# A decoder trunk on one core: x's turns as threads, the last eight weight tiles kept, small products joined

## The chip, the cores and the metric

One core of a Trainium2 chip runs the whole program. The metric is device microseconds per execution: the median of three timed runs. Beside it stands one profiled execution, from which all durations come. The engines are PE (TensorE matmul; PEld is its weight load), DVE (VectorE), ACT (ScalarE), POOL (GpSimd) and SP (SyncE, which here only issues DMAs); each works through its own instructions in program order.

## The reference, cut to what matters

One layer on x of 256 tokens by 2048 channels, all float32:

```python
h = rmsnorm(x, norm_mix_w)
proj = h @ w_in                      # q, k, v, z, b, a, p_in, g_a, g_b
q, k, v = split(silu(causal_dwconv([q, k, v], conv_qkv_w)))
o = gated_delta_rule(l2norm(q), l2norm(k), v, g_log, beta)      # 16 heads of 128
y_a = rmsnorm(o, gdn_norm_w) * silu(z)
y_b = (causal_multiscale_pool(p_in) @ pool_w) * pool_scale
x = x + (sigmoid(g_a) * y_a + sigmoid(g_b) * y_b) @ w_out
gate, up = split(rmsnorm(x, norm_ffn_w) @ w_up)
x = x + (gelu(causal_dwconv(gate, conv_ffn_w) + conv_ffn_b) * up) @ w_down
return rmsnorm(x, norm_final_w)
```

## The kernel before

**The big products.** Every large product is computed in float32 accuracy by three passes of a rounded type: a matrix A is split into a rounded part (hi) and a rest (lo), and hi*hi + lo*hi + hi*lo is summed in PSUM. A weight tile is 256 rows by 512 columns (512 KB). `fetch` (L275) loads it into `raw` (four buffers) on SP's queue, `cast` (L284) makes `whi` on ACT, `split` (L292) makes `wlo` on DVE (`whi` and `wlo` have four buffers each, `wpool`). `weights` (L317) gives the next tile; casts run up to `AHEAD` = 3 tiles in front of the one in use, and fetches up to four tiles in front of the splits. One tile feeds 12 matmuls of 128x512: two k blocks, two token halves (t = 0, 1), three passes. Eight tiles make one product of 2048 by 512 (`gemm_a`, L327), a "step" being one tile.

**The order of the work.** The program's order on each engine is written out by hand, by a small planner at build time. `Plan` (L32) keeps a modelled time for every engine and one for the DMA queue: `dma` (L50) adds a transfer's bytes at 240 KB per us, starting at time 0. Side work is written as generators ("threads"), spawned with a rank; `side` (L205), called after each k block of a big product, first emits what the weight pipeline can do and then the next piece of any thread that the plan holds to be ready. A piece names its engine by `yield "PE"`, `yield "A"` (ACT), `"V"` (DVE), `"G"` (POOL), `"S"` (SP). `until` (L236) repeats this until a condition holds. `bank` (L157) and `leave` hand out the two PSUM buffers `psb`; `pa` gives the two buffers `psa`, `pm` the large ones `psm`.

**The start.** Loads of x (four tiles) and of the first four weight tiles go out alternately (L396 to L401). nmrows, the first norm's weights, is turned on PE into `nmw`. `x_turned` (L411) turns two 128-row blocks of x by four PE transposes, ACT evicts them as `xhi` with the scale, DVE makes `xlo`. `x_turned(0)` is called before the first big product (L1049), and `x_next(c)`, called ahead of step c, calls `x_turned(c + 1)` (L1058): it emits all three engines' parts at once.

**Small products on PE.** In `gdn` (L682; four head groups) the inverse of a triangular block is put together from 32 to 64 to 128 rows: for each of two head pairs (hp) a product `pu` is made on PE, evicted as `u` on ACT, and then the next pair's (L773 and L804). The products that follow (`px`) are made for both pairs at once. `pooled` (L898) multiplies by band matrices, `mixing` (L937) and `residual` (L1105) transpose; each does its work in two halves, PE then ACT then DVE, one bank at a time.

**The end.** The down projection accumulates eight banks: `acc[c][t]`, four column blocks c of 512 and two token halves t. For each row pair kp of 22 and each c, a tile feeds both t (L1232). In the last row pair, c = 0 is done for both halves, then c = 1, 2, 3 for t = 0, then the first half's end is emitted, then c = 1, 2, 3 for t = 1 and the second half's end (L1245 to L1267). An end is: four adds on DVE and four sums of squares on ACT, a reduce and a scale on DVE, a power on POOL (`rs`), scaling by `rs` and by the final weights `nfin` (two columns on DVE, two on ACT), and four stores of 256 KB on SP's queue.

Of the kernel before, what the change touches and what calls it, by code (L numbers as in the profile page):

```python
# [13 lines left out]
P = 128  # L14
# [17 lines left out]
class Plan:  # L32
# [75 lines left out]
def kernel(  # L108
# [163 lines left out]
    def soon(eng, time):  # L272
        return time <= max(now["PE"], now[eng])

    def fetch():  # L275
        i = len(raws)
        src = srcs[i]
        raw = wpool.tile(list(src.shape), F32, tag="raw", name=nm("raw"), bufs=4)
        plan.at(free[i - 4] if i >= 4 else 0.0)
        nc.sync.dma_start(raw, src)  # L280
        landed.append(plan.ready)
        raws.append(raw)

    def cast():  # L284
        i = len(rounded)
        hi = wpool.tile(list(raws[i].shape), F32R, tag="whi", name=nm("whi"))
        plan.at(max(landed[i], now["PE"] if i > AHEAD else 0.0))
        nc.scalar.copy(hi, raws[i])
        cast_at.append(plan.ready)
        rounded.append(hi)  # L290

    def split():  # L292
        i = len(made)
        raw, hi = raws[i], rounded[i]
        plan.at(max(cast_at[i], now["PE"] if i > AHEAD else 0.0))
        if hi.shape[1] == 8:
            lo = None
            nc.vector.tensor_tensor(hi[:, :, 32:64], raw[:, :, 0:32], hi[:, :, 0:32].bitcast(F32), op=ALU.subtract)
        else:
            lo = wpool.tile(list(raw.shape), F32R, tag="wlo", name=nm("wlo"))  # L300
# [95 lines left out]
    for c in range(4):  # L396
# [4 lines left out]
        fetch()  # L401

    plan.at(nmready)
# [5 lines left out]
    xhi, xlo = xhl[:, :, 0, :], xhl[:, :, 1, :]  # L409

    def x_turned(k2):  # L411
        pt = (pa if k2 % 2 else pb)([P, 2, S])
        plan.at(x0[k2 // 2][1])
        for kk in range(2):
            k = 2 * k2 + kk
            for t in range(2):
                nc.tensor.transpose(pt[:, kk, t * P : (t + 1) * P], x0[k // 4][0][:, t, (k % 4) * P : (k % 4 + 1) * P],
                                    ident)
        for kk in range(2):
            k = 2 * k2 + kk  # L420
            nc.scalar.activation(xhi[:, k, :], pt[:, kk, :], AF.Copy, scale=nmw[:, k : k + 1])
        for kk in range(2):
# [259 lines left out]
    def gdn(g, kq, vts, dec0, dec1, res):  # L682
# [88 lines left out]
        pairs = [(slice(o, o + 32), slice(o + 32, o + 64)) for o in (0, 64)]  # L771
        U = []
        for hp in range(2):  # L773
            yield "PE"
            pu = pa([P, 2, 2, 32])
            for t, i in probs:
                for lo, up in pairs:
                    mm(pu[up, t, i, :], lt(2 * hp + i, t)[lo, up], T[hp][lo, t, i, lo], start=True, stop=True)
            u = mp.tile([P, 2, 2, 32], F32, tag="U", bufs=2, name=nm("U"))
            yield "A"  # L780
            for lo, up in pairs:
                nc.scalar.copy(u[up], pu[up])
            U.append(u)
# [18 lines left out]
        lo, up = slice(0, 64), slice(64, 128)  # L802
        U = []
        for hp in range(2):  # L804
            yield "PE"
            pu = pa([P, 2, 2, 64])
            for t, i in probs:
                mm(pu[up, t, i, :], lt(2 * hp + i, t)[lo, up], T[hp][lo, t, i, lo], start=True, stop=True)
            u = mp.tile([P, 2, 2, 64], F32, tag="U", bufs=2, name=nm("U"))
            yield "A"  # L810
            nc.scalar.copy(u[up], pu[up])
            U.append(u)
# [85 lines left out]
    def pooled(e, g, phi, plo):  # L898
        for f2 in range(2):
            yield "PE"  # L900
            n = yield from bank()
            pt = pb([P, 2, S])
            for ff in range(2):
# [3 lines left out]
                mm(pt[:, ff, 0 : P + PAD], e[:, 0, fs], bands[:, g, 0 : P + PAD], start=False, stop=True,  # L907
                   skip_group_check=True)
            fs = slice(2 * f2, 2 * f2 + 2)
            yield "A"  # L910
# [26 lines left out]
    def mixing(g, sz, ps, psb, tb, res, mh, ml):  # L937
# [10 lines left out]
        give("th")  # L948
        for f2 in range(2):
            yield "PE"  # L950
            n = yield from bank()
            pt = pb([P, 2, S])
# [4 lines left out]
            if f2:  # L957
                give("sz")
            fs = slice(2 * f2, 2 * f2 + 2)
# [42 lines left out]
    for g in range(4):  # L1002
# [57 lines left out]

# [44 lines left out]
    def residual(c, ps):  # L1105
# [7 lines left out]
        for k2 in range(2):  # L1113
            yield "PE"
            n = yield from bank()
            pt = pb([P, 2, S])
            for kk in range(2):
                k = 4 * c + 2 * k2 + kk
                for t in range(2):
                    nc.tensor.transpose(pt[:, kk, t * P : (t + 1) * P], xt[:, t, k * P : (k + 1) * P], ident)  # L1120
            yield "A"
            for kk in range(2):
# [106 lines left out]

    LAST = KF // 2 - 1  # L1230
    nfin = None
    for kp in range(LAST + 1):  # L1232
        for c in range(4 if kp < LAST else 1):
            w = weights()
# [4 lines left out]
        if kp == 12:  # L1239
            until(lambda: not threads)  # L1240
            nfin = big.tile([P, D], F32, tag="xhl", name="nfin")
            nc.scalar.dma_start(nfin, norm_final_w.partition_broadcast(P))
    ws = [weights() for c in range(3)]
    ssq5 = cpool.tile([P, 2, 4], F32, name="ssq5")
    for t in range(2):  # L1245
        for c in range(1, 4):
            down_part(LAST, c, t, *ws[c - 1])
        for c in range(4):
            xs = xt[:, t, c * 512 : (c + 1) * 512]
            nc.vector.tensor_tensor(xs, xs, acc[c][t], op=ALU.add)  # L1250
            jk = cpool.tile([P, 512], F32, tag="sqj", name=nm("sqj"))
            nc.scalar.activation(jk, xs, AF.Square, accum_out=ssq5[:, t, c : c + 1])
# [4 lines left out]
        for c in (2, 3):  # L1257
            xs = xt[:, t, c * 512 : (c + 1) * 512]
            nc.vector.tensor_tensor(xs, xs, nfin[:, c * 512 : (c + 1) * 512], op=ALU.mult)
        for c in (0, 2, 1, 3):  # L1260
            xs = xt[:, t, c * 512 : (c + 1) * 512]
            if c < 2:
                nc.vector.scalar_tensor_tensor(xs, xs, rs, nfin[:, c * 512 : (c + 1) * 512],
                                               op0=ALU.mult, op1=ALU.mult)
            else:
                nc.scalar.activation(xs, xs, AF.Copy, scale=rs)
            nc.sync.dma_start(out[0, t * P : (t + 1) * P, c * 512 : (c + 1) * 512], xs)  # L1267

# [30 lines left out]
```

## Time and profile before

| | us |
|---|---|
| median of three runs | 1567.35 (1565.99 to 1568.28) |
| profiled execution, its own time | 1567.87 |
| its span, first to last instruction | 1566.1 |
| PE busy in the span | 1540.2 |
| DVE busy | 1036.6 |
| ACT busy | 787.2 |
| POOL busy | 68.0 |

PE is busy in 98% of the span; busy time counts a matmul's whole modelled length, and successive ones overlap. The mean DMA rate is 213 GB/s, with 333.52 MB moved. Almost every instruction is recorded at line L94, the helper through which the planner issues, so the profile is read by tiles (`whi`, `xhl`, `psm`) and by time, not by line.

### The profile page before, as it was taken

To read this page: it belongs to the slowest core of one execution; us is meant where nothing else is said; L and a number is where in the kernel's file an instruction comes from. 1 tells how busy PE (TensorE), PEld (TensorE's weight loads), DVE (VectorE), ACT (ScalarE), POOL (GpSimd) and SP (SyncE) were. 2 spreads that over 40 slices of the span, in tenths; PEclk is the share of its full clock that TensorE was granted. 3 is DMA by queue.
4 is the path that set the end of the run, shared out by engine and by line. 5 is a ranking of instruction groups with operands and counts; after the bars stand their busy time and mean duration, and the time that the engine had idled before them with its cause. 6 is when DMAs were issued, how large, how long until landed. Compare 5 with 4: busy or idle time off the path is not lost.

```text
span 1566.1 us, 19803 instructions
## 1 busy us (share of the span) xinstructions
PE 1540.2 (98%) x7212; PEld 1261.8 (81%) x7212; DVE 1036.6 (66%) x1488; ACT 787.2 (50%) x1036; POOL 68.0 (4%) x109
## 2 busy tenths in 40 slices
PE   7999999999999999999999999999999999999996
PEld 5787788787878887888888888888888888888885
DVE  4778967788778766865565666666667666544444
ACT  6474574456545854454454445454454444433334
POOL 1201000100010001000000000000000000000000
PEclk9999999999999999999999999999999999999998
DMA  7887974788568857774756888888888887665663
GB/s 227 218 257 191 264 205 140 182 253 245 147 188 234 239 162 202 191 205 133 252 179 187 246 230 233 247 248 250 243 231 232 255 244 210 233 197 191 220 195 110
DMA packets 342585, 333.52 MB, mean 213 GB/s; under 512 B 181031, under 2 KB 201559, under 8 KB 342359
## 3 DMA queue, kind: packets, MB, share of 16 engines
q1 hardware_dynamic: 339776, 327.78, 72.0%
q10 hardware_dynamic: 2710, 4.48, 0.8%
q8 instruction: 56, 0.92, 0.2%
q14 instruction: 43, 0.34, 0.1%
HBM read 309.11 MB, written 23.10 MB: 212 GB/s over the span
## 4 chain that ended last, share of the span: by engine, by line
PE 92%; DVE 3%; DMA 2%; ACT 1%; SPq 1%; issue 1%; DVEq 0%; ACTq 0%
PE psm L94 79%; PE psa L94 8%; PE psb L94 5%; DMA raw<-in_w_in_dram 2%; DVE wlo L94 1%; DVE tmp L94 1%; SPq L94 1%; DVE tb L94 1%; ACT whi L94 0%; DVE xt L94 0%; DVE tn L94 0%; DMA x<-in_x_dram 0%; ACT sqj L94 0%; DVE cy L94 0%; ACT ev L94 0%
## 5 line engine op out<-in xcount | busy, mean ns | idle before, releaser
L94 DVE TENSOR_TENSOR wlo<-raw,whi 128x1024 fp32r<-128x1024 f32 x528 | 641.4, 1222 | 409.7 <-ACT whi L94 404.2
L94 ACT CAST whi<-raw 128x1024 fp32r<-128x1024 f32 x530 | 555.7, 1052 | 621.9 <-PE psm L94 452.2
L94 PE MATMUL psm<-whi,xhl 128*128 128x512 f32 x1792 | 566.8, 398 | 4.3 <-ACT whi L94 4.0
L94 PE MATMUL psm<-whi,fhl 128*128 128x512 f32 x1408 | 433.6, 389 | 0.0
L94 PEld LDWEIGHTS psm<-whi,xhl 128*128 128x128 f32 x1792 | 334.7, 190 | 75.3 <-ACT whi L94 5.1
L94 PE MATMUL psm<-wlo,xhl 128*128 128x512 f32 x896 | 352.7, 394 | 4.2 <-DVE wlo L94 4.2
L94 PEld LDWEIGHTS psm<-whi,fhl 128*128 128x128 f32 x1408 | 264.1, 188 | 54.9
L94 PE MATMUL psm<-wlo,fhl 128*128 128x512 f32 x704 | 273.9, 389 | 0.0
L94 PEld LDWEIGHTS psm<-wlo,xhl 128*128 128x128 f32 x896 | 169.6, 189 | 43.3 <-DVE wlo L94 7.0
L94 PEld LDWEIGHTS psm<-wlo,fhl 128*128 128x128 f32 x704 | 132.1, 188 | 27.4
L94 PE MATMUL psm<-whi,hhi 128*128 128x512 f32 x176 | 68.5, 389 | 0.0
L94 PE MATMUL psm<-whi,hlo 128*128 128x512 f32 x176 | 68.5, 389 | 0.0
L94 PE MATMUL psm<-wlo,hhi 128*128 128x512 f32 x176 | 68.5, 389 | 0.0
L94 ACT ACTIVATE fev<-psm,rs 128x512 f32<-128x512 f32 x44 | 27.9, 686 | 46.2 <-PE psm L94 46.2
L94 PE MATMUL psm<-whi,mhi 128*128 128x512 f32 x128 | 50.5, 394 | 0.0
L94 PE MATMUL psm<-wlo,mhi 128*128 128x512 f32 x128 | 50.0, 390 | 0.0
L94 PE MATMUL psm<-whi,mlo 128*128 128x512 f32 x128 | 49.9, 390 | 0.0
L94 DVE SCALAR_TENSOR_TENSOR cy<-kq,cqw,cy 128x255 f32<-128x255 f32 (+2 forms) x96 | 44.1, 479 | 1.6
L94 DVE SCALAR_TENSOR_TENSOR y<-gs,cfw,y 128x255 f32<-128x255 f32 x88 | 42.6, 484 | 3.1
L94 DVE TENSOR_TENSOR tmp<-lb,tb 128x248 f32<-128x248 f32 (+30 forms) x124 | 37.1, 299 | 4.7 <-DMA lb<-cdd 1.8
L94 DVE TENSOR_TENSOR tb<-tb,tmp 128x248 f32<-128x248 f32 (+30 forms) x124 | 37.3, 301 | 4.3
L94 DVE STREAM_TRANSPOSE tn<-fev 128x1024 f32<-128x1024 f32 x22 | 27.3, 1242 | 17.1 <-ACT fev L94 15.2
(194 smaller groups left out, 1238.2 us busy)
## 6 DMA issues: line engine op xcount, KB each, us to landing
raw<-in_w_in_dram SPq DMA_DIRECT2D x226, 512.0 KB, 4.6
raw<-in_w_up_dram SPq DMA_DIRECT2D x176, 512.0 KB, 4.9
raw<-in_w_down_dram SPq DMA_DIRECT2D x88, 512.0 KB, 4.5
flip<-tn SPq DMA_DIRECT2D x136, 128.0 KB, 3.3
raw<-in_w_out_dram SPq DMA_DIRECT2D x32, 512.0 KB, 4.3
gs<-flip SPq DMA_DIRECT2D x11, 512.0 KB, 5.9
us<-flip SPq DMA_DIRECT2D x11, 512.0 KB, 6.6
kq<-flip SPq DMA_DIRECT2D x8, 512.0 KB, 6.4
```

Of the source, the lines that this page charges most:

```text
L94: r = getattr(self.eng, op)(out, *args, **kw)
```

## The change

Six parts, as the diff has them:

```diff
-        self.queue = 0.0
+        self.queue = 2.5
...
-        self.queue = max(self.queue, self.t[eng]) + n / 240e3
+        self.queue = max(self.queue, self.t[eng]) + n / (170e3 if out.shape[-1] <= 32 else 380e3)
```
The planner's DMA queue starts at 2.5 us, and counts 170 KB per us for transfers whose last dimension is at most 32 elements, and 380 KB per us for others.

```diff
+    tc.nc.scalar.copy(epsx[:, 0:1], epsx[:, 0:1])
+    run_up(6)
     plan.at(nmready)
...
     nc.vector.tensor_copy(nmw, pv[:, :KD])
+    run_up(3)
...
     def x_turned(k2):
+        yield "PE"
+        while len(turned) < k2 - 3:
+            yield
+        n = yield from bank()
...
+        leave(n)
+        turned.append(plan.ready)
...
-            x_turned(0)
+            for k2 in range(8):
+                plan.at(x0[k2 // 2][1])
+                spawn(x_turned(k2), -3)
...
             def x_next(c):
+                until(lambda: len(turned) > c)
...
-                if c < 7:
-                    x_turned(c + 1)
```
`run_up(n)` issues n products `ones` by `ones` (128x128) into an unused bank. The copy is ACT's first instruction. The eight turns become threads of the highest rank, each due when its part of x has arrived; step c waits, in the plan, for turn c.

```diff
-        for hp in range(2):
-            yield "PE"
+        yield "PE"
+        pus = []
+        for hp in range(2):
             pu = pa([P, 2, 2, 32])
+            pus.append(pu)
             ...
+        for pu in pus:
+            yield "A"
             u = mp.tile([P, 2, 2, 32], F32, tag="U", bufs=2, name=nm("U"))
```
In both merges of `gdn` (32 and 64 rows) the products of both head pairs are issued in one piece, and the evictions follow.

```diff
+    def both():
+        yield "PE"
+        pair = []
+        for _ in range(2):
+            n = yield from bank()
+            pair.append((n, pb([P, 2, S])))
+        return pair
```
`pooled`, `mixing` and `residual` take two banks by `both()`, issue both halves' PE work in one piece, and then evict half by half.

```diff
+    def keep(i):
+        j = i - (len(srcs) - 4 * KEPT)
+        return last[0][:, j] if 0 <= j < 4 * KEPT - 4 else None
...
+    for kp in range(ROWS - KEPT, ROWS):
+        for c in range(4):
+            kept.append((kp, c, *weights()))
+            down_part(kp, c, 0, *kept[-1][2:])
+            side()
...
+    for c in range(4):
+        added(0, c)
+    turn(0)
+    for c in range(2):
+        weighed(0, c)
+    turn(1)
+    added(1, 0)
+    finish(0)
+    turn(2)
+    weighed(1, 0)
+    added(1, 1)
+    turn(3)
+    weighed(1, 1)
+    added(1, 2)
+    added(1, 3)
+    finish(1)
```
With `KEPT` = 2, the last two row pairs (eight tiles) are used for t = 0 only as they come, and stay: the first four in a tile `last` at the place of `xhl`, the other four in the ring's buffers. Then `turn(c)` does t = 1 for column block c from the kept tiles, 12 matmuls each. `added` is the add and the sum of squares, `weighed` the product with the final weights, which lie in two tiles at the places of `gs` and `y`, loaded by two transfers on ACT's queue.

```diff
+        for c in (3, 0, 2, 1):
+            xs = xt[:, t, c * 512 : (c + 1) * 512]
+            to = out[0, t * P : (t + 1) * P, c * 512 : (c + 1) * 512]
+            if c in (0, 1):
+                nc.scalar.activation(xs, xs, AF.Copy, scale=rs)
+                nc.scalar.dma_start(to, xs)
+            elif c == 2:
+                nc.vector.tensor_scalar(xs, xs, rs, None, op0=ALU.mult)
+                nc.sync.dma_start(to, xs)
+            else:
+                nc.vector.scalar_tensor_tensor(xs, xs, rs, nfin[1][:, 1], op0=ALU.mult, op1=ALU.mult)
+                nc.sync.dma_start(to, xs)
```
In `finish(t)` two columns are scaled on ACT and stored by ACT's queue, two are scaled on DVE and stored by SP's.

More of the change, by code (lines that the diff above doesn't have):

```diff
@@ L299, in split @@
         else:
-            lo = wpool.tile(list(raw.shape), F32R, tag="wlo", name=nm("wlo"))
+            lo = keep(i)
+            lo = wpool.tile(list(raw.shape), F32R, tag="wlo", name=nm("wlo")) if lo is None else lo[:, 1]
             nc.vector.tensor_tensor(lo, raw, hi.bitcast(F32), op=ALU.subtract)
@@ L401, with run_up @@
         fetch()
+    def run_up(n):
+        warm = pa()
+        for _ in range(n):
+            tc.nc.tensor.matmul(warm[:, 0:P], ones, ones, start=True, stop=True)
+    tc.nc.scalar.copy(epsx[:, 0:1], epsx[:, 0:1])
+    run_up(6)
     plan.at(nmready)
@@ L898, in pooled @@
     def pooled(e, g, phi, plo):
[L899 to L902, printed above, removed]
+        pair = yield from both()
+        for f2, (n, pt) in enumerate(pair):
             for ff in range(2):
@@ L908, in pooled @@
                    skip_group_check=True)
+        for f2, (n, pt) in enumerate(pair):
             fs = slice(2 * f2, 2 * f2 + 2)
@@ L948, in mixing @@
         give("th")
[L949 to L952, printed above, removed]
+        pair = yield from both()
+        for f2, (n, pt) in enumerate(pair):
             for ff in range(2):
@@ L956, in mixing @@
                     nc.tensor.transpose(pt[:, ff, t * P : (t + 1) * P], sz[:, t, f * P : (f + 1) * P], ident)
-            if f2:
-                give("sz")
+        give("sz")
+        for f2, (n, pt) in enumerate(pair):
             fs = slice(2 * f2, 2 * f2 + 2)
@@ L1112, in residual @@
             nc.scalar.activation(jk, xs[:, t, :], AF.Square, accum_out=ssq4[:, t, c : c + 1])
[L1113 to L1116, printed above, removed]
+        pair = yield from both()
+        for k2, (n, pt) in enumerate(pair):
             for kk in range(2):
@@ L1120, in residual @@
                     nc.tensor.transpose(pt[:, kk, t * P : (t + 1) * P], xt[:, t, k * P : (k + 1) * P], ident)
+        for k2, (n, pt) in enumerate(pair):
             yield "A"
@@ L1240, with added, weighed, finish @@
             until(lambda: not threads)
-            nfin = big.tile([P, D], F32, tag="xhl", name="nfin")
-            nc.scalar.dma_start(nfin, norm_final_w.partition_broadcast(P))
-    ws = [weights() for c in range(3)]
-    ssq5 = cpool.tile([P, 2, 4], F32, name="ssq5")
[L1245 to L1252, printed above, removed]
+            last.append(big.tile([P, 4, 2, 2, 512], F32R, tag="xhl", name="last"))
+            for n, tag in enumerate(("gs", "y")):
+                nfin.append(fp.tile([P, 2, 512], F32, tag=tag, name=f"nfin{n}"))
+                nc.scalar.dma_start(nfin[n].rearrange("p c d -> p (c d)"),
+                                    norm_final_w[n * 1024 : (n + 1) * 1024].partition_broadcast(P))
+    kept = []
+    for kp in range(ROWS - KEPT, ROWS):
[3 more added lines that the diff above has]
+            side()
+    ssq5 = cpool.tile([P, 2, 4], F32, name="ssq5")
+    def added(t, c):
+        xs = xt[:, t, c * 512 : (c + 1) * 512]
+        nc.vector.tensor_tensor(xs, xs, acc[c][t], op=ALU.add)
+        jk = cpool.tile([P, 512], F32, tag="sqj", name=nm("sqj"))
+        nc.scalar.activation(jk, xs, AF.Square, accum_out=ssq5[:, t, c : c + 1])
+    def weighed(t, c):
+        xs = xt[:, t, c * 512 : (c + 1) * 512]
+        nc.vector.tensor_tensor(xs, xs, nfin[c // 2][:, c % 2], op=ALU.mult)
+    def finish(t):
         rs = cpool.tile([P, 1], F32, name=nm("rs"))
```

39 lines of the change are left out of this document (21 added, 18 removed).

## The prediction

> **What bounds the kernel now.** I read the page first (span, chain of waits), then the chain in order of time, the waits of PE, the stretches where PE isn't dense, and the timeline there.
>
> ```profile
> span 1566.1 us, 19803 instructions
> ...
> PE 92%; DVE 3%; DMA 2%; ACT 1%; SPq 1%; issue 1%; DVEq 0%; ACTq 0%
> ...
> 843.03 471.96 PE psm L94 x2082
> ```
> PE is the bound: 92% of the chain. The last row (chain in order of time) gives its pace: 2082 matmuls of 128x512 in 471.96 us, 0.2267 us each. Nothing in the change removes such a matmul, so a gain can come only from where PE is not at that pace. Two such stretches (columns: length, busy time of PE, PEld, DVE, ACT, POOL, then clock, DMA share, GB/s):
>
> ```profile
> 9.60:22.35 12.75, 10.60 (x33) 7.29 (x33) 4.45 (x5) 5.51 (x12) 0.00 (x0) 0.87 0.71 246
> ...
> 164.70:174.50 9.80, 6.65 (x17) 4.86 (x17) 9.32 (x20) 6.83 (x18) 0.00 (x0) 0.65 0.93 245
> ```
> Start: PE is hardly used before 9.6, then slow to 22.35. Middle: 17 matmuls take 9.80 us instead of 17 x 0.2267 = 3.85, so one stall costs 5.9 us. The third is the end, where PE's last matmul starts at 1553.97 and the span goes on for 12.1 us; its rows stand below. Between them PE waits nowhere for 1 us.
>
> **Start: x's turns as threads, run-up.** The timeline of PE, ACT and DVE before:
>
> ```profile
> 5.78 1.12 PE L94 MATMUL psb<-ident,x 128*128 128x128 f32 x4 [1.48 <-DMA x<-in_x_dram]
> ...
> 9.61 1.22 PE L94 MATMUL psm<-whi,xhl 128*128 128x512 f32 x2 [1.86 <-ACT whi L94]
> 10.87 0.79 PE L94 MATMUL psm<-wlo,xhl 128*128 128x512 f32 x1
> 11.46 1.05 PE L94 MATMUL psm<-whi,xhl 128*128 128x512 f32 x2
> ...
> 14.02 0.66 PE L94 MATMUL psm<-whi,xhl 128*128 128x512 f32 x2
> ...
> 14.76 0.60 PE L94 MATMUL psb<-ident,x 128*128 128x128 f32 x4
> 17.22 1.03 PE L94 MATMUL psm<-whi,xhl 128*128 128x512 f32 x2 [1.86 <-ACT whi L94]
> ...
> 22.35 0.71 PE L94 MATMUL psm<-whi,xhl 128*128 128x512 f32 x2
> ...
> 8.52 1.04 ACT L94 CAST whi<-raw 128x1024 fp32r<-128x1024 f32 x1
> 15.39 0.84 ACT L94 ACTIVATE xhl<-psb,nmw 128x256 fp32r<-128x256 f32 x2 [5.83 <-PE psb L94]
> 16.12 1.99 ACT L94 CAST whi<-raw 128x1024 fp32r<-128x1024 f32 x2
> ...
> 6.00:15.50 9.50, 7.45 (x24) 5.22 (x23) 2.95 (x5) 2.72 (x6) 0.00 (x0) 1.00 1.05 393
> ```
> What is seen: ACT waits 5.83 us for the turn at 14.76, which stands in PE's order behind the whole first step, and the cast of the second weight tile stands in ACT's order behind that turn. The tile had long landed: the eight first transfers of 524 KB run at 393 GB/s (last row), 1.33 us each; the fourth is there near 10 (an estimate from that rate). PE starves from 15.4 to 17.22, and the half-clock pace (two matmuls and their start-to-start near 0.43 us, as at 11.46) comes back from 17.22 on.
>
> In the change all eight turns are threads ahead of everything, planned at x's arrival, and a step waits only for its own turn. By the code, turns 2 and 3 land after the sixth matmul of step 0, and the cast of tile 1 stands ahead of their evictions. Sum: the first cast still ends at 9.56 (two evictions of 0.84, then 1.04), so the first matmul stays near 9.6 and the first wlo near 10.87. From there 10 + 12 matmuls and two turns of 0.45 remain to step 2: 22 x 0.2267 + 0.9 = 5.9 us. At full clock step 2 starts at 16.8, against 22.35: 5.5 us. If the clock rises only where it did before, at the pair of 14.02, the 3.2 us to there do 1.6 us of that work, and step 2 starts at 18.4: 4.0 us. If one eviction still delays tile 1 by the old 1.86 us, 2.1 us. I take **4.5 us**, bounds 2.1 and 5.5: nearer the row as it was, because PE will idle from the last turn (near 8) to 9.6 whatever warms it. Past step 2 nothing holds it: a step and a turn are 2.72 + 0.45 on PE, 1.33 on DMA, and on ACT a cast, a turn's evictions and a square, 1.04 + 0.84 + 0.63 (the square as at 1551.10, below).
>
> The run-up's nine products are 18 records on PE. The nearest row is the fp32 128x128 product:
>
> ```profile
> L94 PE MATMUL psa<-w,ga 128*128 128x128 f32 x128 | 15.6, 275 | 0.0
> ```
> 0.122 us per record, twice that at half clock: 4.4 us, laid into 1.0 to 5.8, when PE waits for nmrows (4.04) and x. Cost nothing; if it runs over, the turn at 5.78 is late by some 0.3 us. The early table load takes 1.28 us off an ACT that is idle until 6.93: nothing.
>
> [...]
>
> **Joined products.** The chain in order of time:
>
> ```profile
> 542.25 0.37 PE psa L94 x16
> 542.62 2.94 PE psm L94 x12
> ...
> 551.59 0.62 PE psa L94 x32
> ...
> 558.71 0.60 PE psa L94 x8
> ...
> 562.26 1.07 PE psa L94 x16
> ...
> 788.92 0.44 PE psb L94 x4
> ...
> 793.48 0.87 PE psb L94 x8
> ```
> The 12 matmuls behind a small group take 2.94 us instead of 12 x 0.2267 = 2.72: each change back costs 0.22. First merge: two groups cost 2 x (0.37 + 0.22) = 1.18; joined, like the group of 32 at 551.59, 0.62 + 0.22 = 0.84. Saved 0.34. Second merge: 2 x (0.60 + 0.22) = 1.64 against 1.07 + 0.22 = 1.29 (562.26, the 16 records of the same size). Saved 0.35. Four head groups: **2.8 us**, bounds 0 (the 32 and 16 there have other operands) and 3.0. Turns gain nothing: four cost 0.44, eight 0.87, so the fixed part is at most 0.01 and the mixing and residual pairs (eight) and the bands (four) together give 0.1. Asking for two banks at once can make PE wait for an eviction with the big stream queued behind it; today no wait of PE on psb's readers appears, so I put it at nothing, at worst one 0.84 us ACT eviction in a few of twelve pairs.
>
> **End.**
>
> ```profile
> 1549.89 0.39 PE L94 MATMUL psm<-wlo,hhi 128*128 128x512 f32 x1
> ...
> 1553.97 0.39 PE L94 MATMUL psm<-wlo,hhi 128*128 128x512 f32 x1
> ...
> 1550.32 0.69 DVE L94 TENSOR_TENSOR xt<-xt,psm 128x512 f32<-128x512 f32 x1 [0.67 <-PE psm L94]
> ...
> 1551.10 0.63 ACT L94 ACTIVATE sqj<-xt 128x512 f32<-128x512 f32 x1 [0.64 <-DVE xt L94]
> 1551.86 0.16 DVE L94 TENSOR_REDUCE rs<-ssq 128x1 f32<-128x4 f32 x1 [0.85 <-ACT sqj L94]
> 1552.28 0.93 POOL L94 TENSOR_TENSOR rs<-rs,epsx 128x1 f32<-128x1 f32 x1 [706.38 <-DVE rs L94]
> ...
> 1559.83 1.33 ACT L94 ACTIVATE xt<-xt,rs 128x512 f32<-128x512 f32 x2 [1.42 <-POOL rs L94]
> ...
> 1554.09 8.37 SPq L94 DMA_DIRECT2D out_dram<-xt  x8
> ```
> Before, all four columns of the second half end together, and four adds and four squares queue up: rs is used from 1559.83 on, 5.86 us after the last matmul's start at 1553.97. After, only the last column is left: add 0.43 us after its last matmul (1549.89 to 1550.32), square 0.78 later, reduce 0.76 later, then 0.42 to POOL and 0.97 from its start to ACT's: 3.36. Gain 2.5. From there to the end took 6.3 us: four of SP's eight issues in a row, 1 MB of output. Two columns go to ACT's queue, which also issues between its two scalings (one scaling waits behind the other's issue); on SP one of DVE's two multiplications loses an operand (bounds 0.3 and 0.74 us). I take 0.6, bounds 0 and 1. Together **3.1 us**, bounds 2.2 and 3.6. The first half's adds, scalings and output (about 8 us of DVE) lie beside the last 10.9 us of PE (48 matmuls); were that cover gone, they would show as a late start of the last add. The final weights, now two transfers of half the size, still start nine rows of four tiles ahead: 9 x 4 x 2.72 = 98 us.
>
> The price is a faster weight stream: the last eight tiles are used for t=0 alone, 6 x 0.2267 = 1.36 us each instead of 2.72.
>
> ```profile
> raw<-in_w_down_dram SPq DMA_DIRECT2D x88, 512.0 KB, 4.5
> ...
> L94 DVE TENSOR_TENSOR wlo<-raw,whi 128x1024 fp32r<-128x1024 f32 x528 | 641.4, 1222 | 409.7 <-ACT whi L94 404.2
> ```
> Four raw buffers through landing 4.5, cast 1.04 and split 1.22 give one tile per 1.7 us. But up to seven tiles are fetched ahead, and four of the eight go into the kept tile and wait for no buffer of the ring. I put it at nothing, at worst 8 x 0.34 = 2.7 us.
>
> **The planner's new rates.** They change no instruction but the order of them, on SP above all. The stall in the middle:
>
> ```profile
> 168.30 0.79 PE L94 MATMUL psm<-wlo,xhl 128*128 128x512 f32 x1 [3.15 <-DVE wlo L94]
> ...
> 159.15 1.28 ACT L94 ACT_TABLE_LOAD   x1 [2.39 <-DMA dec<-rund]
> ...
> 163.33 1.98 ACT L94 CAST whi<-raw 128x1024 fp32r<-128x1024 f32 x2
> ...
> 157.00 6.62 SPq L94 DMA_DIRECT2D back<-tb  x4
> ...
> PE psm L94 <- DVE wlo L94: 4.2, 4, 3.2
> ```
> The last row (waits of PE: total, times, longest) says that this one wait is 3.2 of all 4.2 us that PE spent on a split. The casts stand behind the decays, which waited for a late transfer; SP is held 6.62 us by four narrow ones. A plan that gives narrow transfers 170 instead of 240 KB per us and wide ones 380 knows of that lateness, but not of SP's being held. Nothing in the trace shows the new order: bounds from +5.9 (a second such stall) to -5.9 (it goes). I take **-2 us**, a third of it.
>
> **Sum.** 4.5 + 2.8 + 0.1 + 3.1 + 2.0 = 12.5 against the profiled execution's own 1567.87 us (span 1566.1): 1555.4. The median shown, 1567.35, lies 0.5 lower, so the forecast for it is **1555.0 us**.
>
> **Rivals.** (1) The stall goes whole: 3.9 us more, 1551.1. For it: it began with a misjudged arrival. Against: DMA is at 0.93 of its share there. (2) The weights of the end run dry: 1555.0 + 2.7 = 1557.7. Against: the lead of seven. (3) The new order opens one more stall: 1560.9. (4) Slower: the burst of narrow transfers stalls PE in the three other head groups too, as it does in the first; 3 x 5.9 = 17.7, 1572.7; it decides from the third stall (12.4 + 3.1 eaten). Against: all other waits for a split are 1.0 us together, the start's among them. (5) The clock does not rise at the run-up: 0.5 more, 1555.5, inside the forecast.
>
> Chances: forecast, with (5), 0.48 (its own range 1552.5 to 1558); (1) 0.25; (2) 0.10; (3) 0.12; (4) 0.05. About 0.2% (3.1 us) is what a measurement of this kernel can tell from no change. Faster by more: 0.91, as (3) with a small start could come within; same 0.04; slower 0.05, which is (4). The range takes in (1) with the start's and end's upper bounds to one side and (3) to the other: 1549 to 1562.
>
> **What would show it.** Step 2's first matmul at 16.8 to 18.4; the step's matmuls with no gap between the first wlo and there; 32 and 16 records in one group for the two merges; last matmul to end 9 us instead of 12.1; the clock row and DVE's wait near 160. The forecast is wrong if the plan moves a cast behind a late transfer elsewhere, or if PE waits for whi in the last 22 us.

## The result and the profile after

| | before | after |
|---|---|---|
| median (lowest to highest, runs) | 1567.77 (1565.99 to 1568.28, 4) | 1554.59 (1551.80 to 1557.09, 4) |
| ratio to before, 95% interval | | 0.9917 [0.9905, 0.9929] |
| profiled execution, its own time | 1567.87 | 1553.68 |
| its span | 1566.1 | 1552.0 |
| start of PE's last matmul | 1553.97 | 1542.52 |
| from there to the end of the span | 12.16 | 9.45 |

The change takes 13.2 us off the median; 1555.0 was forecast, with 1549 to 1562 as its range. The page of the kernel after, first its span, then busy times, then the engines' shares of the chain that ended last:

```profile
span 1552.0 us, 19823 instructions
...
PE 1534.5 (99%) x7230; PEld 1260.5 (81%) x7230; DVE 1038.6 (67%) x1490; ACT 787.8 (51%) x1037; POOL 69.4 (4%) x109
...
PE 91%; DMA 4%; DVE 2%; ACT 2%; issue 1%; SPq 0%; ACTq 0%; POOLq 0%; POOL 0%; DVEq 0%
```

PE is still the bound, with nearly the same share of the chain. Its pace in the dense part, from the chain of the kernel after in order of time, is the old one: 2100 matmuls in 476.01 us are 0.2267 us each.

```profile
827.53 476.01 PE psm L94 x2100
```

So the gain lies where PE was not dense. The same two stretches of time as before, and a third that turned out to matter (columns as in the prediction: length, busy time of PE, PEld, DVE, ACT, POOL, clock, DMA share, GB/s), kernel after:

```profile
9.60:22.35 12.75, 12.62 (x63) 10.28 (x63) 9.55 (x14) 11.38 (x21) 0.00 (x0) 1.00 0.97 333
164.70:174.50 9.80, 8.72 (x39) 6.90 (x38) 9.10 (x15) 4.21 (x5) 0.00 (x0) 1.00 0.87 229
...
320.00:345.00 25.00, 22.74 (x97) 17.59 (x96) 21.80 (x40) 19.54 (x38) 1.32 (x2) 1.00 0.94 297
```

The third stretch of the kernel before:

```profile
320.00:345.00 25.00, 25.00 (x112) 20.71 (x111) 22.82 (x45) 13.04 (x16) 2.06 (x2) 1.00 0.95 280
```

PE's records (the xN in brackets, small products and turns among them) are 63 in the stretch of the start where 33 were, at a clock of 1.00 instead of 0.87. At 165 to 174, 39 stand where 17 stood, at 1.00 instead of 0.65. But at 320 to 345, 97 stand where 112 stood: there PE has become worse.

How the lead grows shows where the time came from. For matmul n of the 6352 of 128x512, counted from 0, the table takes its start in the profile before less its start in the profile after:

```
matmul n   at (after)  lead us
24 (step 2)     16      5.97
95              35      5.25
580            155      5.91
620            164     12.82     the stall of before is gone
720            190     10.09     waits at 167 and 179
1000           268     10.81
1300           343      7.49     waits at 321 and 334
2400           630     10.49
last          1542     11.45
end of span   1552      14.16
```

By parts: the start 5.25 (5.91 if the steps up to matmul 580 are counted with it); the joined merges 2.73, from their own rows below; the end 14.16 - 11.45 = 2.7; and what is left of the 11.45, about 3.5, is put down to the planner's new order, with some 0.1 of pairs in it. That last part is a remainder of one profile and not a measurement of its own.

**The start.** PE, then ACT, in the timeline of the kernel after:

```profile
1.05 2.93 PE L423 MATMUL psa<-ones 128*128 128x128 f32 x12 [1.05 <-POOL ones L94]
...
5.84 0.60 PE L94 MATMUL psa<-ident,x 128*128 128x128 f32 x4
8.46 0.73 PE L94 MATMUL psm<-whi,xhl 128*128 128x512 f32 x2 [2.02 <-ACT whi L94]
...
16.38 0.62 PE L94 MATMUL psm<-whi,xhl 128*128 128x512 f32 x2
```

```profile
6.04 0.84 ACT L94 ACTIVATE xhl<-psb,nmw 128x256 fp32r<-128x256 f32 x2 [3.28 <-PE psb L94]
7.37 1.04 ACT L94 CAST whi<-raw 128x1024 fp32r<-128x1024 f32 x1 [0.48 <-DMA raw<-in_w_in_dram]
8.32 0.84 ACT L94 ACTIVATE xhl<-psa,nmw 128x256 fp32r<-128x256 f32 x2
```

Four turns take 0.60 us at 5.84, against 1.12 at 5.78 before: the clock is up already. The first cast stands between the evictions of turns 0 and 1 and not behind both, so the first matmul comes at 8.46; step 2 begins at 16.38.

**The merges.** The chain of the kernel after has each merge in one group, at the length of the group of 32 or 16 that stood next to it before:

```profile
534.74 0.62 PE psa L94 x32
535.36 5.66 PE psm L94 x24
541.03 1.07 PE psa L94 x16
...
774.94 0.87 PE psb L94 x8
```

The 24 matmuls behind the first group take 5.66 instead of 24 x 0.2267 = 5.44: one change back of 0.22, where there were two. Measured as the time added to the big matmuls around them, the two merges cost 0.84 and 1.29, and 1.17 and 1.64 before: 0.68 us. Taken for all four head groups this is 2.73; in two of them the second merge stood, before and after, partly beside other small products, so that the figure is an estimate there.

**The end.** The timeline of the kernel after, behind the last matmul at 1542.52:

```profile
1542.94 0.69 DVE L94 TENSOR_TENSOR xt<-xt,psm 128x512 f32<-128x512 f32 x1 [1.74 <-PE psm L94]
...
1545.87 0.72 ACT L94 ACTIVATE xt<-xt,rs 128x512 f32<-128x512 f32 x1 [1.42 <-POOL rs L94]
...
1547.04 0.72 ACT L94 ACTIVATE xt<-xt,rs 128x512 f32<-128x512 f32 x1 [0.45 <-ACT xt L94]
```

One add and one square stand between the last matmul and the scaling: 1545.87 - 1542.52 = 3.35 us, where it was 5.86. From there to the end it is 6.1, where it was 6.3.

**What is left as waits.** What PE waited for in the kernel after (total, times, longest), and the two longest places in its timeline:

```profile
PE psm L94 <- ACT whi L94: 3.4, 3, 2.0
PE psm L94 <- DVE wlo L94: 3.2, 5, 1.1
```

```profile
167.89 0.50 PE L94 MATMUL psm<-wlo,xhl 128*128 128x512 f32 x1 [1.08 <-DVE wlo L94]
...
334.22 0.73 PE L94 MATMUL psm<-whi,xhl 128*128 128x512 f32 x2 [1.15 <-ACT whi L94]
```

The 2.0 is the start's. The wait of 3.15 us at 168 is down to 1.08, and the clock there is 1.00 where it was 0.65. A new one has opened at 334.

### The profile page after: what moved, and what is told of

It is laid out like the page before. It is cut to its first block, busy times and chain, and to the rows that moved or that the text cites. A ratio compares the mean times of both kernels' runs of the same rounds, so it can differ in the third digit from the quotient of the medians.

```text
span 1552.0 us, 19823 instructions
## 1 busy us (share of the span) xinstructions
PE 1534.5 (99%) x7230; PEld 1260.5 (81%) x7230; DVE 1038.6 (67%) x1490; ACT 787.8 (51%) x1037; POOL 69.4 (4%) x109
## 4 chain that ended last, share of the span: by engine, by line
PE 91%; DMA 4%; DVE 2%; ACT 2%; issue 1%; SPq 0%; ACTq 0%; POOLq 0%; POOL 0%; DVEq 0%
PE psm L94 79%; PE psa L94 7%; PE psb L94 5%; DMA raw<-in_w_in_dram 3%; ACT whi L94 1%; DVE wlo L94 1%; SPq L94 0%; DVE cy L94 0%; DMA kq<-flip 0%; ACT junk L94 0%; DVE tmp L94 0%; ACT xhl L94 0%; DVE tb L94 0%; ACTq L94 0%; ACT xt L94 0%
## 5 line engine op out<-in xcount | busy, mean ns | idle before, releaser
L94 PEld LDWEIGHTS psm<-whi,hhi 128*128 128x128 f32 x168 | 31.6, 188 | 6.7
```

What stands on the lines that cost most here:

```text
L94: r = getattr(self.eng, op)(out, *args, **kw)
```

## The experiments

Times are medians with lowest, highest and the number of runs; each ratio is to runs of the kernel before on the same chip, whose medians lay between 1565.6 and 1567.7, and differences of some 2 us and less between experiments on different chips are not sure. "Lead" is the table's, against the profile of before.

**How much one kernel's plan varies.** The changed kernel, unedited, once more (a0).

> The changed kernel as it is, a second time, as the base of the runs beside it. Expected within the four times already seen, 1551.8 to 1557.1 us. If the stalls of the first two head groups (3.4 and 3.2 us of waits for a cast and a split, in the first profile) lie at other places or have other lengths here, the spread of 5 us comes from them; if they are the same to a few tenths, it comes from elsewhere.

1554.85 (1553.32 to 1556.06, 5), 0.9926 [0.9913, 0.9939]. Its profile has waits at the same places, 166, 181, 323 and 334, but of other lengths: the lead at matmul 720 is 8.3 instead of 10.1, and at the last one 9.7 instead of 11.45. A single profile of this kernel can thus be off by up to 2 us in the region from 160 to 340. That accounts for some 2 of the 5 us over which its times spread.

The start varies too. The edits of e3, e4, e10 and e13 below change nothing before 40 us, so with a0 there are six profiles of one and the same start:

```
profile   step 2 at   lead at matmul 95   clock at half, from to
after       16.38           5.25          -
a0          17.04           5.12           8.26  11.67
e3          17.73           4.47           9.58  12.99
e4          17.68           4.54           9.48  12.89
e10         17.74           4.44           9.61  13.02
e13         18.14           3.99          10.33  13.74
```

In five of the six the clock falls once more, around the first matmuls, each time for 3.41 us; only in the profile of after it does not. The start is thus worth 4.0 to 5.25, 4.6 in the mean, and the 5.25 above is the best of six. What follows compares medians first and uses profiles to say where.

**The run-up out** (e2).

```diff
-    run_up(6)
-    run_up(3)
```

> Only the nine products of the run-up are left out; they are not in the plan, so the order of everything else is the same. Theory: the run-up lifts the clock before the first step. Without it the first matmuls of 128x512 run at 0.43 us apart until some 11 to 14 us, step 2 starts 1.5 to 2.5 us later than 16.4, and the median is 1556 to 1557 us. Rival: the turns and the first matmuls lift the clock by themselves, or it falls in the gap before the first matmul either way; then step 2 starts within 0.5 us of 16.4 and the median is the same as that of the changed kernel.

1555.84 (1554.84 to 1558.20, 5), 0.9936 [0.9923, 0.9950]: 1.0 us above a0, with intervals that overlap. The timeline of PE without run-up:

```profile
8.53 1.22 PE L94 MATMUL psm<-whi,xhl 128*128 128x512 f32 x2 [1.01 <-ACT whi L94]
```

The first matmul comes at 8.53 all the same, at half pace (1.22 for two, against 0.73). Step 2 comes at 18.51, 0.4 to 2.1 us later than in the six profiles above, and the lead at matmul 95, 3.69, is 0.3 to 1.6 below theirs, 0.9 in the mean. So the threads carry most of the start, and the run-up about one microsecond of it, which the medians alone don't tell from nothing.

**Do transposes warm PE?** First the run-up made of transposes, 10 and 4 (e6).

```diff
-            tc.nc.tensor.matmul(warm[:, 0:P], ones, ones, start=True, stop=True)
+            tc.nc.tensor.transpose(warm[:, 0:P], ones, ident)
...
-    run_up(6)
+    run_up(10)
...
-    run_up(3)
+    run_up(4)
```

> The run-up is made of 10 and 4 transposes of 128x128 instead of 6 and 3 products, about as long on PE at half clock (0.27 us each). [...]

1554.63 (1554.10 to 1556.26, 4), 0.9923 [0.9907, 0.9940]. The pace stayed at half until 12.8 (1.05 for two matmuls at 10.57, 0.62 at 13.44; until 14.6 without a run-up), but the run-up ended before x was there and left PE idle for 0.46 us, so the run does not tell whether the transposes or the gap held it there. Hence a longer one, 11 and 8, in one run (e9):

> [...]

1554.03 in one run. Its timeline of PE:

```profile
1.42 2.61 PE L423 MATMUL psa<-ident,ones 128*128 128x128 f32 x11 [1.42 <-POOL epsx L94]
...
4.24 1.97 PE L423 MATMUL psa<-ident,ones 128*128 128x128 f32 x8
...
6.54 0.60 PE L94 MATMUL psa<-ident,x 128*128 128x128 f32 x4
...
10.41 1.05 PE L94 MATMUL psm<-whi,xhl 128*128 128x512 f32 x2
```

Nothing but transposes ran before the first matmul of 128x512, and the turns of x at 6.54 go at 0.60 for four, against 1.06 for the same turns in e6: in this run transposes alone lifted the clock. That it fell again at 9.6 (1.05 for two) is another matter, taken up in the last section.

**The bridge** (e12). Does it help to keep PE warm from the turns to the first matmul?

```diff
                 until(lambda: len(turned) > c)
+                if c == 0:
+                    run_up(7)
```

> Seven more products of ones, some 1.7 us, between the first turns and the first matmul, where PE waits 1.9 us for the first cast. Theory: in executions where the clock falls back there (it did in one of two profiles of the changed kernel, at 8.26 us, and step 2 was 0.7 us later) it now stays up; step 2 starts at 16.2 to 16.6 us and the median is 0.3 to 0.7 us lower, 1554.2. Rival: the products run over and push the first matmul; then it starts later than 8.5 us.

1554.26 (1553.04 to 1555.65, 5), 0.9924 [0.9910, 0.9937]. The median is the theory's, but 0.6 below a0 with intervals that overlap is no gain shown. PE keeps the full pace from the turns on (0.61 for four at 5.51, 0.73 for the first two matmuls at 8.39) and step 2 starts at 16.28, yet the lead at matmul 95 is 4.4, no more than in the profiles where the clock fell: the time is lost again in a wait of 1.31 us for `xhl` before 23.91, on DVE behind a split whose cast waited 0.85 for its weight tile. With PE warm, the tiles' arrival, ACT and DVE set the pace of the first product.

**Turns in their old places** (e8), with the run-up kept: `x_turned(0)` ahead, then `x_turned(c + 1)` inside step c.

```diff
-            for k2 in range(8):
-                plan.at(x0[k2 // 2][1])
-                spawn(x_turned(k2), -3)
+            x_turned(0)
...
-                until(lambda: len(turned) > c)
...
+                if c < 7:
+                    x_turned(c + 1)
```

> The turns of x are issued in place again, one step ahead and all three engines at once, as before the change; run-up, rates and all else stay. Theory: the threads are what takes the cast of the second weight tile out from behind the third turn. In place, PE waits again for whi for 1 to 2 us between the first two steps, step 2 starts at 19 to 20.5 us instead of 16.4 to 17, and the median is 1557 to 1559 us. Rival: at full clock the third turn comes early enough that the cast loses little; then step 2 starts before 18 us and the median stays below 1556 us.

1561.17 (1557.35 to 1562.53, 6), 0.9960 [0.9945, 0.9974]: 6.3 us above a0. PE, ACT and DVE in its timeline:

```profile
18.42 0.71 PE L94 MATMUL psm<-whi,xhl 128*128 128x512 f32 x2
22.61 0.80 PE L94 MATMUL psm<-wlo,xhl 128*128 128x512 f32 x1 [3.48 <-DVE wlo L94]
```

```profile
10.07 1.05 ACT L94 CAST whi<-raw 128x1024 fp32r<-128x1024 f32 x1 [1.30 <-DMA raw<-in_w_in_dram]
15.50 0.84 ACT L94 ACTIVATE xhl<-psb,nmw 128x256 fp32r<-128x256 f32 x2 [4.38 <-PE psb L94]
...
19.68 0.84 ACT L94 ACTIVATE xhl<-psa,nmw 128x256 fp32r<-128x256 f32 x2
```

```profile
20.55 0.88 DVE L94 SCALAR_TENSOR_TENSOR xhl<-psa,nmw,xhl 128x256 fp32r<-128x256 f32 x2 [3.30 <-ACT xhl L94]
```

The median is above the theory's, and its mechanism is not what is seen. The cast of the second tile stands at 10.07, ahead of the turn, although the turns are in place; PE does not wait for it, and step 2 comes at 18.42, before the forecast 19. The loss comes one step later. ACT idles 4.38 us for the third turn, the casts of the next tiles follow it, the fourth turn's eviction stands behind them at 19.68, and DVE waits 3.30 us for that eviction with the splits of those tiles behind it. So the split is 3.48 us late at 22.61, and the clock behind it is at half (0.80 for one matmul, against 0.50 behind the same wait in e7 below). The lead at matmul 95 is -1.96 instead of 5.25. What the threads save is this second knot, on DVE.

**The old rates under the rest** (e1), and **the new rates alone** in the kernel before (e7). The edit is e1's; e7's is its reverse:

```diff
-        self.queue = 2.5
+        self.queue = 0.0
...
-        self.queue = max(self.queue, self.t[eng]) + n / (170e3 if out.shape[-1] <= 32 else 380e3)
+        self.queue = max(self.queue, self.t[eng]) + n / 240e3
```

> The planner's old DMA rate and start (240 KB per us, 0) under the rest of the change. Theory: the new rates gave the part of the gain that is neither in the start, the merges nor the end, 3.4 us between the two profiles (5.5 us at the stall of 164 us, less 2 us of new ones after it); with the old rates a wait of PE of 3 us or more for a split comes back in the first head group, with a fall of the clock, and the median is 1557 to 1560 us. Rival: the stall went because the rest of the change moved PE by 6 us against the transfers; then the median stays at 1554 to 1555.5 us.

> The kernel before with only the planner's new rates and start. Theory: the rates act by themselves, on the stall of the first head group: the median is 3 to 5 us under that of the kernel before, 1563 to 1565 us, and no wait of PE for a split reaches 2 us. Rival: they help only together with the earlier start of the big matmuls; then the median is within 1.5 us of 1567.7 us or above it, and a wait of 3 us stays.

Old rates: 1559.62 (1557.65 to 1561.57, 5), 0.9956 [0.9943, 0.9970], 4.8 us above a0. New rates alone: 1568.04 (1566.22 to 1570.69, 10), 1.0010 [1.0001, 1.0019], no gain. The median of e1 is the theory's, but the place is not: the stall did not come back at 164, where it had been; between matmuls 580 and 620 the lead grows by 6.9 as in the kernel after. PE's timeline of the kernel with the old rates:

```profile
337.15 0.73 PE L94 MATMUL psm<-whi,xhl 128*128 128x512 f32 x2 [1.60 <-ACT whi L94]
339.90 0.79 PE L94 MATMUL psm<-wlo,xhl 128*128 128x512 f32 x1 [2.02 <-DVE wlo L94]
```

Two waits at 337 to 340 and then half clock (1.05 for two matmuls at 340.49): the lead falls from 11.4 at matmul 1000 to 3.7 at 1340. The kernel with the rates alone does lose the stall of 164 (its lead grows by 6 up to matmul 600), but has paid for it:

```profile
22.20 0.50 PE L94 MATMUL psm<-wlo,xhl 128*128 128x512 f32 x1 [3.47 <-DVE wlo L94]
```

The same wait as in e8, and at 340 its lead falls again, from 4.7 to 0.4. So at the start the new rates need the threads. They move the casts (the second tile's is at 9.98 in e7, before at 16.12), and with the turns in place the splits then wait. The threads do not need the rates there: the lead at matmul 95 is 5.35 in e1, with that cast at 10.01. And the stall of 164 goes in e1 without the new rates and in e7 without the rest; either is enough, and which shift of the order does it was not traced.

**The old end** (e3), with no kept tiles.

> The end as before the change: no kept tiles, the last row pair c by c, the second half's four adds and squares after the last matmul, all stores by SP. Theory: last matmul to end takes 12.1 us again instead of 9.45, the median is 2 to 3 us above the changed kernel's, 1557 to 1558 us. Rival: the kept tiles cost PE waits in the last 22 us that eat part of it (none is seen in the profile of the changed kernel); then the lead at the start of the last matmul grows by what they cost.

1557.55 (1556.66 to 1558.74, 4), 0.9947 [0.9930, 0.9963]: 2.7 us above a0. Its last matmul starts at 1542.83 and the span ends at 1555.0, 12.2 later, as before; its lead there, 11.14, is the kernel after's 11.45 within the spread. The kept tiles cost PE nothing, and the end is worth its 2.7.

**The merges pair by pair again** (e4), everything else kept.

```diff
-        yield "PE"
-        pus = []
         for hp in range(2):
+            yield "PE"
             pu = pa([P, 2, 2, 32])
-            pus.append(pu)
...
-        for pu in pus:
             yield "A"
```

> Both merges of the head groups issue their products pair by pair again. Theory: each costs one change back to the big matmuls more, 0.33 and 0.36 us, four times: 2.7 us, median 1557 to 1558 us, and the lead over the kernel before shrinks by 0.7 us at each of four places. Rival: the plan moves with it and the stalls of the first head groups change by as much or more; then the groups cost as said, but the median is not 2 to 3.5 us up.

1558.84 (1557.30 to 1560.05, 4), 0.9952 [0.9937, 0.9967]: 4.0 us above a0, more than the 2.7 that its rows bear out: the rival. The chain of this kernel has the groups as before:

```profile
534.98 0.37 PE psa L94 x16
```

The rest is, by its profile, in the region near 334: a wait of 2.6 us for a cast and a clock of 0.86 from 320 to 345. Splitting a merge also moves everything planned behind it. The pairs of `both()` were not undone on their own; their rows (0.87 for eight, as before) leave them no more than the 0.1 forecast.

**Narrow stores on POOL's queue** (e10). The waits left at 167, 179 and 334 have a common look. SP in the timeline of the kernel after:

```profile
154.98 5.05 SPq L94 DMA_DIRECT2D back<-tb  x4
...
166.76 4.54 SPq L94 DMA_DIRECT2D flip<-tn  x4
171.40 3.02 SPq L94 DMA_DIRECT2D raw<-in_w_in_dram  x4
...
320.40 6.92 SPq L94 DMA_DIRECT2D flip<-tn  x4
```

and ACT, which waits 7.11 us for the first of the tiles fetched at 171.40:

```profile
177.76 1.05 ACT L94 CAST whi<-raw 128x1024 fp32r<-128x1024 f32 x1 [7.11 <-DMA raw<-in_w_in_dram]
```

Four stores in 128-byte pieces hold SP for 4.5 to 6.9 us, and three or four weight fetches queue behind each burst: from 160.13 on, behind `back`, those of the wait at 167; from 171.40 those of the waits at 179 and 180; from 327.42 those of the wait at 334. If that is the cause, stores issued elsewhere should free the fetches:

```diff
-        yield "S"
+        yield "G" if pool is mp else "S"
...
-            nc.sync.dma_start(dv[a], b[32 * a : 32 * a + 32].rearrange("p t (f j) -> p t f j", j=32))
+            (nc.gpsimd if pool is mp else nc.sync).dma_start(dv[a], b[32 * a : 32 * a + 32].rearrange("p t (f j) -> p t f j", j=32))
...
-        yield "S"
+        yield "G"
...
-            nc.sync.dma_start(dv[a], b[32 * a : 32 * a + 32].rearrange("p h (n j) -> p h n j", j=32))
+            nc.gpsimd.dma_start(dv[a], b[32 * a : 32 * a + 32].rearrange("p h (n j) -> p h n j", j=32))
```

> The narrow stores of the flips and of the flips back in the first part (four each, 128 KB in 128-byte pieces) are issued by POOL instead of SP; nothing else. Theory: what is left of PE's waits near 166 to 181 and 321 to 335 us (3.1 to 5.2 us together in the profiles so far) comes from SP, which is held 4.5 us by four such stores while weight fetches stand behind them; then these waits fall under 1.5 us together and the median is 1550 to 1552 us. Rival: the DMA engines themselves are full there (share 0.9 and more), and the weights come no earlier whoever issues; then the waits stay within 1 us of what they were and the median is 1554 to 1556 us. A store issued by POOL may also land later, which would lengthen the threads.

**1550.97** (1550.56 to 1551.23, 4), 0.9903 [0.9889, 0.9916]: all four runs lie below the lowest of the nine runs of the changed kernel (1551.80), and they spread over 0.7 us where those spread over 5. This is the fastest version here. How far it leads the changed kernel is less sure: that kernel's nine runs are from other chips, and the ratios to before (0.9903 against 0.9917 and 0.9926) have intervals that overlap a little. The nearest kernel timed beside it on the same chip is e12, 1553.04 to 1555.65, 3.3 us above it by the medians. POOL and SP in its timeline:

```profile
164.81 3.23 POOL L94 DMA_DIRECT2D flip<-tn  x4 [7.15 <-DVE tmp L94]
...
168.07 3.88 SPq L94 DMA_DIRECT2D raw<-in_w_in_dram  x4
```

The fetches go out at 168.07 instead of 171.40, and the waits of PE between 160 and 345 are

```profile
168.10 0.50 PE L94 MATMUL psm<-wlo,xhl 128*128 128x512 f32 x1 [0.47 <-DVE wlo L94]
...
338.31 0.50 PE L94 MATMUL psm<-wlo,xhl 128*128 128x512 f32 x1 [1.49 <-DVE wlo L94]
```

2.0 us in all, where the kernel after has 4.1 and a0 5.8. That is the theory's direction and time, though not its 1.5 us: the weights' waits are halved and not gone. Its stores' way, from issue to landing (last column, median us), by the queue that issues them:

```profile
flip<-tn SPq DMA_DIRECT2D x88, 128.0 KB, 3.5
flip<-tn POOLq DMA_DIRECT2D x48, 128.0 KB, 5.7
```

Such a store takes longer to land from POOL here, 5.7 us against 3.5; but these stores have time, and what stood behind them on SP had none.

**More of the same: the loads of `lb` on POOL too** (e13).

```diff
-        yield "S"
+        yield "G"
...
-            nc.sync.dma_start(lb[32 * cq : 32 * cq + 32], cdd.rearrange("q (r j) i -> (q r) j i", j=B0))
+            nc.gpsimd.dma_start(lb[32 * cq : 32 * cq + 32], cdd.rearrange("q (r j) i -> (q r) j i", j=B0))
```

> As e10_flips_pool, and the four loads of lb in 128-byte pieces also go by POOL. Theory: SP held by narrow transfers is what delayed the weights; lb was the last such burst on SP in this part (2.1 us for four), so the waits of PE from 100 us to 720 us fall below the 2.3 us of e10_flips_pool and the median is 1549 to 1551 us. Rival: what is left there is DVE and ACT order (a split behind the substitution, a cast behind the decays, as at 336 us), which this does not touch; then the median is the same to 1 us, 1550 to 1552.

1553.12 (1551.44 to 1557.12, 5), 0.9918 [0.9904, 0.9931]: above both the theory's and the rival's time, and 2.2 us above the stores alone, with intervals that overlap a little. The profile is of the slowest of the five runs. POOL, DVE and PE in its timeline:

```profile
155.44 3.52 POOL L94 DMA_DIRECT2D back<-tb  x4 [4.38 <-DVE tb L94]
...
166.69 1.25 DVE L94 STREAM_TRANSPOSE tn<-ev 128x1024 f32<-128x1024 f32 x1 [3.16 <-DMA back<-tb]
...
171.52 0.80 PE L94 MATMUL psm<-wlo,xhl 128*128 128x512 f32 x1 [3.45 <-DVE wlo L94]
```

A `back` store that lands late holds a transpose on DVE for 3.16 us, the splits stand behind it, and PE waits 3.45, about as long as before the change. The loads of `lb` did not stand in the way of that store on POOL, which had been idle for 4.38 us when it came to these stores. Why it landed late, and whether the loads had a part in it, stays open.

## Why the prediction came true, and where it missed

**The bound** was read rightly: PE's pace did not change, and the gain came from the start, the merges, the end and the stall in the middle.

**The start**, 4.5 forecast, 5.25 measured at matmul 95 in the profile of after, 4.6 in the mean of six. Step 2 came at 16.38 there, below the forecast 16.8 to 18.4, and at 17.04 to 18.14 in the other five, inside it: which of them one reads is luck, as the clock stayed up in one alone. What failed is the step that the first cast still ends at 9.56 behind two evictions. The plan put it between them, and the first matmul came 1.15 us earlier. With that order and no run-up it still comes 1.08 earlier (8.53 in e2); with the run-up and the cast behind both evictions, 0.80 (8.81 in e1). The price of a cold clock was set at 1.5 us between the two cases; against the one profile in which it stayed up, the five in which it fell are 0.7 to 1.8 later at step 2 and 0.1 to 1.3 at matmul 95. That the threads take the second tile's cast out from behind the third turn is true (10.01 in e1, under the old rates), but the new rates do so by themselves (e7, e8), and the turns in place then cost their time on DVE. That PE idles from the last turn to the first matmul whatever warms it was right; e12 shows that filling the gap brings nothing at matmul 95. The sentence that past step 2 nothing holds the first product was too strong: the wait of 1.31 us in e12 is one that a tile, ACT and DVE make.

**Joined products**, 2.8 + 0.1 forecast: 2.73 by the rows. The working (each group's own length and 0.22 for each change back) held to 0.07. In the median, undoing them costs 4.0 (e4), since the plan behind them shifts too.

**The end**, 3.1 forecast, 2.7 by the spans and 2.7 by e3. The 3.36 from the last matmul to the scaling came out at 3.35. The term that was mis-sized is the stores: 0.6 forecast, 0.2 measured. The output went out at 376 and 380 GB/s from 1547.5 to 1550.0, and before at 381 and 346 from 1561.8 to 1564.0, so the second queue brought it out hardly faster. ACT's second scaling waited 0.45 behind its own store's issue, as feared. That the kept tiles cost nothing was right (e3).

**The planner**, 2.0 forecast as a third of the stall, about 3.5 left for it in the profile of after, 1.8 by the same count in a0. The step that failed is the third of one stall, a choice with no row behind it. Both rivals to it happened: the stall went whole, as in (1), and the lead grows by 6.9 from matmul 580 to 620; and others opened, as in (3), which take 2.7 of it at 167 and 179 and 3.3 at 321 and 334. The stall is not the rates' alone to remove, as it goes in e1 too. What the sum missed is that the term does not stand by itself: alone the new rates gain nothing (e7), and without them the rest loses 4.8 (e1), at 337 and not at 164. Undone one at a time, rates, turns, end, merges and run-up cost 4.8, 6.3, 2.7, 4.0 and 1.0, together 18.8 for a change that gained 13.2. That the sum came out within 0.4 us is in part luck: the end was put too high by 0.4, the planner too low by up to 1.5, and the kernel's own runs spread over 5 us.

**The slower rival** (4), three more stalls, did not come; the one at 334 is the kind it spoke of. Its reason, that narrow transfers hold SP, is supported by e10, which removes part of those waits by moving the stores. Whether SP's freed queue alone did that, or also the cheaper transfers of the last section, was not separated.

## What to carry to other kernels

Look at the engine whose queue is in program order for work that waits on something late while ready work stands behind it: ACT's casts behind a turn, weight fetches behind narrow stores, splits behind a turn or a transpose were one and the same pattern, and time came back where the waiter was moved. Price small interruptions of a dense PE stream as their own length plus a fixed cost for each change back (0.22 us here), and join them. When the order is made by a model, don't expect the gains of single edits to add up: each edit moves the plan. And read a short stretch, such as the start here, from several profiles before naming its price.

## What the hardware showed that was not expected

**The clock fell while PE was busy for about half of the time.** In a0 it is at half from 8.26 to 11.67, in the kernel before from 17.48 to 20.89. That fall in a0, with the 3.41 us ahead of it (columns as above):

```profile
4.85:8.26 3.41, 1.63 (x13) 1.20 (x11) 0.88 (x2) 1.77 (x3) 0.92 (x3) 1.00 0.97 334
8.26:11.67 3.41, 3.21 (x7) 1.99 (x8) 1.79 (x2) 1.90 (x4) 0.00 (x0) 0.50 1.05 394
```

PE was busy for 1.63 of 3.41 us, 48%, and then the clock was 0.50. In e9 it was busy for 1.67 of 3.41, 49%, up to the fall at 9.61, and in the kernel before for 1.56 of 3.42, 46%, up to the one at 17.48. In the profile of after it was 1.93 of 3.42, 56%, from 4.33 to 7.75, and the clock column stayed at 1.00. What decides between the two was not shown, nor why the same start lost the clock in five profiles and kept it in one. The clock column does not tell the pace of the start: in e6 it says 1.00 from 5.92 to 9.33, where four turns take 1.06 and the first two matmuls 1.22, against 0.60 and 0.73 in the profile of after.

**The same stores cost DMA less when POOL issued them.** In e10 8.39 MB of 128-byte pieces moved from SP's queue to POOL's. The DMA queues of the kernel after, then of e10 (packets, MB, share of the 16 engines' span):

```profile
q1 hardware_dynamic: 339200, 326.73, 72.4%
```

```profile
q1 hardware_dynamic: 272640, 318.34, 68.0%
q0 software_dynamic: 3072, 8.39, 2.4%
```

SP's queue lost 4.4% and POOL's took 2.4%, in 3072 packets where there had been 66560. POOL pays for it with 3.23 to 3.48 us for each four stores (those at 164.81 and 154.18), on an engine that was busy for 4% of the span in the kernel after.
